# Residual kept scaled by the root of the mean square in the feed-forwards; sum copies placed in the output tile

## The chip, the core and the metric

The kernel runs on one core of a Trainium2 chip. A core has a matrix engine (TensorE, PE in the profile; its weight loads are listed apart as PEld), three engines that work on data in the on-chip memory SBUF (VectorE = DVE, ScalarE = ACT, GpSimd = POOL), and queues that start transfers from the chip's large memory (SP's queue carries most of them here). Matrix products end in a small accumulator memory, PSUM. Each engine takes its instructions strictly in its own order and waits for others through semaphores. The metric is the time of one execution on the device in microseconds (us); the median of several runs counts.

## The reference

The program is an encoder trunk of two layers on 512 tokens with 1024 features, in float32, with 16 learned tokens put in front for the layers and dropped at the end. Each layer adds three things to the residual h:

```python
h = h + 0.5 * swiglu(rmsnorm(h, g[l, 0]), w_gate[l, 0], w_up[l, 0], w_down[l, 0])
h = h + mixer(rmsnorm(h, g[l, 1]), ...)
h = h + 0.5 * swiglu(rmsnorm(h, g[l, 2]), w_gate[l, 1], w_up[l, 1], w_down[l, 1])
...
def rmsnorm(x, g):    # per token
    return x * rsqrt(mean(x * x) + EPS) * g
def swiglu(x, w_gate, w_up, w_down):
    return (silu(x @ w_gate) * (x @ w_up)) @ w_down
```

So there are four feed-forwards (width 2816) and two mixers (a linear-attention branch and a softmax-attention branch, merged by gates). A last rmsnorm gives the output.

## The kernel before

All activations are held transposed: features on the 128 partitions, tokens along the row. The residual `h` is one tile of 8 chunks of 128 features x 528 tokens (512 in the last feed-forward). Every matrix product in full precision is made of three matmuls on halves: each operand is split into a high part (`whi`, `g` and so on) and the rest (`wlo`). For a block of weights ACT makes the high part (L238) and DVE the low part (L239, one instruction of 128x1024).

**The norm.** The gain is multiplied into the operand, but the factor per token, `rs`, is not: products are made from unscaled operands and the factor is put in afterwards. `Norm.rs` (L483) lets PE sum the squares (`means`, L410) and calls `rsqrt_of` (L413), which computes rsqrt with a Newton step; the row `rs` holds -2 times the reciprocal root, hence the factors -0.5 and -0.25 in what follows. Its last two instructions on DVE are L421 and L422.

**A feed-forward** (`ffn`, L507) works through 11 pairs of blocks of 128 hidden features, in three groups of 4, 4 and 3 pairs. For each pair, gate and up products are formed by seven products ("1", "2", "5", "6", "7", "4", "3") in place of eight, each of 24 matmuls of 128x264 (L531), with sums of weight blocks as operands. Those weight sums are made by transfers that add (POOL, L189), fed by loads on SP's queue and, for two of them, by a negation on ACT (L184). The results of the seven products are added up outside PE: ACT copies some PSUM results into a buffer (`snapshot`, L534 to L538, buffer `snap`), DVE adds other PSUM results to them and writes into the tile `c` (L545, L553, L555, L560). `hidden` (L563) then scales gate and up by `rs` (L571; for the up half the scale is left out), takes silu on ACT, multiplies (L577) and splits into `g` high and low (L392, L393).

After each group come the down products (`down`, L580): for each of the 8 chunks of h, matmuls (L404) sum the group's hidden values into PSUM. The up factor was left out, so this sum still lacks one factor per token: `add_to_h` (L496) calls `scaled` (L492, L494), which multiplies PSUM by -0.25 and `rs` into a buffer `t`, and then adds `t` to h (L503). A mixer's output needs no factor and is added straight from PSUM (L499). With the last group's addition a chunk of h is done and the next stage takes it: `chunk` (operand and square, L430 to L442) before a mixer, `pair` (L444) before a feed-forward, `finish_chunk` before the end. Chunks 5 to 7 of the last feed-forward are handled in halves of 256 tokens in `ending` (L1067, L1068).

**Order.** The program is written in a logical order, with weights asked for some products ahead; a scheduler of the framework then fixes the order of instructions on each engine from its own estimates and from priorities. `Norm.rs` runs with high priority. An instruction that needs a buffer waits until the last reader of the buffer's former content is through. Buffers: `g` 16 of 128x528, `t` 6, `rs` 2; for each feed-forward `c` 2 of 128x2112 and `snap` 3 of 128x528; PSUM pools `ss` and `s2` of two tiles each.

Of the kernel before, what the change touches and what calls it, by code (L numbers as in the profile page):

```python
# [17 lines left out]
P = 128  # L18
D = 1024
KC = D // P  # L20
# [255 lines left out]
def build(tc, ctx, xt, wts, win, par, w2, const, umask, out):  # L276
# [10 lines left out]
    slots = {n: pool("s_" + n, b) for n, b in dict(g=16, t=6, rs=2).items()}  # L287
# [27 lines left out]
    def slot(tag, dtype=F32, n=None):  # L315
        return slots[tag].tile([P, T], dtype, tag=tag, name=nm(tag))[:, : n or live[0]]

# [71 lines left out]
    def split(src, tag_hi, tag_lo):  # L389
        n = src.shape[-1]  # L390
        hi, lo = slot(tag_hi, F32R, n), slot(tag_lo, F32R, n)
        S.copy(hi, src)  # L392
        V.tensor_tensor(lo, src, hi.bitcast(F32), ALU.subtract)  # L393
        return hi, lo
# [29 lines left out]
    class Norm:  # L424
# [71 lines left out]
    def add_to_h(m, acc, rs, f):  # L496
        if rs is None:
            for pv, cut in acc.parts:
                V.tensor_tensor(cut(h(m)), cut(h(m)), pv, ALU.add)  # L499
        else:  # L500
            t = slot("t")
            scaled(t, acc, rs, f)
            V.tensor_tensor(h(m), h(m), t, ALU.add)  # L503
# [3 lines left out]
    def ffn(l, f, norm, done, following):  # L507

        x, rs, n = norm.x, None, live[0]
        w = n // 2  # L510
        pools = open_pools("left", psum=("s2",), c=2, snap=3, s2=2)
        made, hid, sums = {}, {}, {}

        def product_of_pair(p, product):
# [19 lines left out]
            def snapshot(name):  # L534
                t = slots["snap"].tile([P, T], F32, tag="snap", name=nm("snap"))[:, :n]
                st[name] = v2(t)
                copied = S.copy(st[name], acc).ins  # L537
                W.behind = copied  # L538

            if product == "1":  # L540
                snapshot("p1")
            elif product == "2":
                c = slots["c"].tile([P, 4 * T], F32, tag="c", name=nm("c"))[:, : 4 * n]
                st["c"] = c.rearrange("p (j q c) -> p j q c", j=2, q=4)
                V.tensor_tensor(st["c"][:, :, 0], st["p1"], acc, ALU.add)  # L545
            elif product == "6":
                snapshot("q")
            elif apart:
                S.copy(st["c"][:, :, 2], acc)
                st["apart"] = True  # L550
            elif product == "7":
                snapshot("r")
                V.tensor_tensor(st["c"][:, :, 3], st["r"], st["Z"][:, :, :w], ALU.add)  # L553
                if "apart" in st:
                    V.tensor_tensor(st["c"][:, :, 2], st["c"][:, :, 2], st["r"], ALU.add)  # L555
                    hidden(st, p, 1)
            elif product == "4":
                hidden(st, p, 1)
            elif product == "3":
                V.tensor_tensor(st["c"][:, :, 1], st["q"], acc, ALU.add)  # L560
                hidden(st, p, 0)

        def hidden(st, p, m):  # L563

            c = st["c"]
            t, u = [c[:, j, 2 * m : 2 * m + 2].rearrange("p q c -> p (q c)") for j in range(2)]
            x21 = st["X"][:, :, :w]
            cuts = [(t, u, t, u, slice(0, n))] if m == 0 or "apart" in st else \
                [(t[:, :w], u[:, :w], x21[:, 0], x21[:, 1], slice(0, w)), (t[:, w:], u[:, w:], t[:, w:], u[:, w:], slice(w, n))]
            for td, _, ts, _, cs in cuts:  # L570
                V.scalar_tensor_tensor(td, ts, -0.5, rs[:, cs], ALU.mult, ALU.mult)  # L571
            act(t, t, AF.Silu)
            if pending:
                with after(prev_act[0]):
                    pending.pop()()
            for _, ud, _, us, cs in cuts:
                V.tensor_tensor(ud, t[:, cs], us, ALU.mult)  # L577
            hid[2 * p + m] = split(u, "g", "g")

        def down(g, m, first, last):  # L580
# [21 lines left out]
        for i, step in enumerate(steps):  # L602
            if step[0] == "P":
# [4 lines left out]
                if step[1:] == (0, "5"):  # L608
                    rs = norm.rs()
# [8 lines left out]
    def project(x, rs, tag, f=1.0, n=T):  # L618
        t = slot(tag, n=n)
# [351 lines left out]
    def mixer(l, norm, done, following):  # L971
# [45 lines left out]
        gates = [project(x, None, "g", n=n_out) for _ in range(EARLY)]  # L1017
        bt = attention(l, x, rs, n_out)
        gates += [project(x, None, "g", n=n_out) for _ in range(2 * KC - EARLY)]
        live[0] = n_out  # L1020
        a = [split(t, "x", "x") for t in sr]
        b = [split(t, "x", "x") for t in bt]
        sig = table("sigmoid_and_others")
        y = []
        for m in range(KC):
# [12 lines left out]
            y.append(split(t, "g", "g"))  # L1038
# [3 lines left out]
        for m in range(KC):  # L1042
            add_to_h(m, product("w_out", Acc(KINDS[m % 4]), y, KC), None, 1.0)
            done(m)
# [12 lines left out]
    def ending(sums, operand, rs):  # L1057
# [144 lines left out]
```

## Time and profile before

| | |
|---|---|
| device time, median of 3 runs | 2235.04 us (2234.63 to 2238.08) |
| span of the profiled execution | 2233.2 us |
| between that span and the median | 1.8 us |
| PE busy | 2196.7 us, 98% |
| DVE busy | 1519.1 us, 68% |
| ACT busy | 1195.1 us, 54% |
| POOL busy | 154.2 us, 7% |
| mean clock granted to PE | 0.998 of full speed |

The profile is of one execution, taken by the hardware; its own device time is its span and what lies around it. Rows of the timeline read: start in us from the begin of the span, duration, engine, line of the kernel, operation, output<-inputs by the program's names (buffer numbers left out), their shapes, how many were merged into the row, and in brackets how long the engine was idle before it and who ended that idle time. Rows of groups give busy us and the mean in ns of one after the bar, then idle us before them. Rows of waits give the waiting engine, tile and line, then whom it waited for, with total us, times and the longest. Rows of stretches give for each engine busy us and the number of its instructions.

Matmuls are pipelined, so a matmul's duration (0.28 us) is longer than the distance from one start to the next (0.12 us).

### The profile page before, as it was taken

Reading aid. Unit: us, or ns where it says so; the run is one execution under the profiler, and the core shown is the slowest. Engines: PE = TensorE matmul, PEld = TensorE weight load, DVE = VectorE, ACT = ScalarE, POOL = GpSimd, SP = SyncE. Lnnn points to the kernel's source line nnn. Section 1 sums busy time; section 2 is a strip of 40 time slices with the busy share of each in tenths; the row PEclk is TensorE's granted clock in tenths of the full one; section 3 lists DMA queues with packets and bytes.
Section 4 is the critical chain, followed back from the end, with each engine's and each line's share of the span. In section 5 each row is a group of like instructions: output and inputs, shape, how many; then the busy total and the mean of one; then the engine's idle time right before and its main releaser. Section 6 shows DMA issues by size and latency. Waiting matters only on the chain.

```text
span 2233.2 us, 39696 instructions
## 1 busy us (share of the span) xinstructions
PE 2196.7 (98%) x16506; PEld 2091.9 (94%) x16506; DVE 1519.1 (68%) x2413; ACT 1195.1 (54%) x1771; POOL 154.2 (7%) x180
## 2 busy tenths in 40 slices
PE   7999999999999999999999999999999999999998
PEld 7999999989999999999999999999788888989897
DVE  7657567586876666565686565675878767756667
ACT  8536355354784564453575353553557836636453
POOL 1111010000000010101011110100000001101010
PEclk9999999999999999999999999999999999999999
DMA  9768563212113486776768686632121146868672
GB/s 275 206 157 221 152 164 106 76 53 72 48 39 114 133 201 168 171 195 154 198 152 207 154 204 167 165 109 77 54 79 48 48 123 156 221 161 207 168 182 67
DMA packets 88612, 315.58 MB, mean 141 GB/s; under 512 B 9840, under 2 KB 12272, under 8 KB 88432
## 3 DMA queue, kind: packets, MB, share of 16 engines
q1 hardware_dynamic: 61136, 218.26, 29.2%
q0 software_dynamic: 25344, 92.29, 23.2%
q8 instruction: 130, 2.13, 0.4%
q10 hardware_dynamic: 1952, 2.50, 0.3%
q14 instruction: 50, 0.41, 0.1%
HBM read 264.77 MB, written 2.10 MB: 120 GB/s over the span
## 4 chain that ended last, share of the span: by engine, by line
PE 79%; DVE 8%; DMA 6%; ACT 5%; issue 2%; SPq 0%; POOL 0%; DVEq 0%; ACTq 0%; POOLq 0%
PE ss L531 30%; PE ss L404 26%; PE mm L404 13%; DMA w<-win 4%; PE sm L404 2%; DVE wlo L239 2%; DMA s<-w 2%; PE sm L916 1%; ACT whi L238 1%; PE ss L891 1%; PE ss L410 1%; ACT t L387 1%; PE sm L932 1%; PE ss L892 1%; PE sm L933 1%
## 5 line engine op out<-in xcount | busy, mean ns | idle before, releaser
L531 PE MATMUL ss<-xc,whi 128*128 128x264 f32 (+1 forms) x4928 | 902.8, 285 | 13.3 <-ACT whi L238 7.4
L531 PEld LDWEIGHTS ss<-xc,whi 128*128 128x128 f32 x4928 | 766.2, 189 | 17.2 <-ACT whi L238 7.6
L531 PE MATMUL ss<-xc,wlo 128*128 128x264 f32 (+1 forms) x2464 | 701.8, 285 | 3.4 <-DVE wlo L239 3.4
L404 PE MATMUL ss<-g,whi 128*128 128x264 f32 (+2 forms) x2692 | 496.8, 300 | 1.6 <-ACT g L392 0.9
L531 PEld LDWEIGHTS ss<-xc,wlo 128*128 128x128 f32 x2464 | 465.7, 189 | 5.2 <-DVE wlo L239 5.0
L404 PEld LDWEIGHTS ss<-g,whi 128*128 128x128 f32 x2692 | 391.6, 188 | 19.1 <-ACT g L392 1.6
L404 PE MATMUL mm<-x,whi 128*128 128x264 f32 (+1 forms) x1712 | 384.7, 315 | 0.0
L239 DVE TENSOR_TENSOR wlo<-w,whi 128x1024 fp32r<-128x1024 f32 (+1 forms) x221 | 268.0, 1217 | 157.2 <-ACT whi L238 157.1
L238 ACT CAST whi<-raw 128x1024 fp32r<-128x1024 f32 x190 | 199.3, 1049 | 246.6 <-PE mm L404 97.5
L238 ACT CAST whi<-w 128x1024 fp32r<-128x1024 f32 (+1 forms) x221 | 229.8, 1046 | 160.0 <-PE ss L404 88.0
L404 PE MATMUL ss<-g,wlo 128*128 128x264 f32 (+2 forms) x1346 | 312.5, 300 | 0.0
L404 PEld LDWEIGHTS mm<-x,whi 128*128 128x128 f32 x1712 | 278.5, 188 | 16.5 <-issue 1.0
L239 DVE TENSOR_TENSOR wlo<-raw,whi 128x1024 fp32r<-128x1024 f32 x190 | 232.0, 1221 | 74.3 <-ACT whi L238 73.9
L404 PE MATMUL mm<-x,wlo 128*128 128x264 f32 (+1 forms) x856 | 266.3, 316 | 0.0
L404 PEld LDWEIGHTS ss<-g,wlo 128*128 128x128 f32 x1346 | 215.8, 188 | 8.2
L537 ACT COPY snap<-ss 128x528 f32<-128x528 f32 (+1 forms) x132 | 78.4, 594 | 221.0 <-PE ss L531 221.0
L404 PEld LDWEIGHTS mm<-x,wlo 128*128 128x128 f32 x856 | 159.7, 188 | 8.4 <-issue 0.7
L494 DVE SCALAR_TENSOR_TENSOR t<-ss,rs 128x528 f32<-128x528 f32 (+1 forms) x93 | 64.5, 701 | 125.5 <-PE ss L404 125.4
L239 DVE TENSOR_TENSOR wlo<-s,whi 128x1024 fp32r<-128x1024 f32 x88 | 107.5, 1222 | 32.9 <-ACT whi L238 32.9
L184 ACT ACTIVATE s<-w 128x1024 f32<-128x1024 f32 x88 | 92.1, 1057 | 53.2 <-DMA w<-win 37.7
L189 POOL DMA_DIRECT2D w<-win x44 | 38.9, 884 | 984.1 <-DMA w<-win 539.9
L238 ACT CAST whi<-s 128x1024 fp32r<-128x1024 f32 x88 | 92.5, 1051 | 0.0
(246 smaller groups left out, 2570.8 us busy)
## 6 DMA issues: line engine op xcount, KB each, us to landing
w<-win SPq DMA_DIRECT2D x219, 512.0 KB, 4.5
raw<-wts SPq DMA_DIRECT2D x190, 512.0 KB, 3.4
s<-win POOLq DMA_DIRECT2D x44, 512.0 KB, 7.1
w<-s POOLq DMA_DIRECT2D x44, 512.0 KB, 5.5
w<-win POOLq DMA_DIRECT2D x44, 512.0 KB, 5.9
s<-w POOLq DMA_DIRECT2D x44, 512.0 KB, 8.0
h<-xt SPq DMA_DIRECT2D x3, 528.0 KB, 6.1
out<-h ACTq DMA_DIRECT2D x4, 256.0 KB, 2.4
```

The source lines that it names most:

```text
L184: self.nc.scalar.activation(t, w, AF.Copy, scale=-1.0)
L189: self.nc.gpsimd.dma_start(t, src, accum_op=ALU.add)
L238: nc.scalar.copy(hi[:, cs], w[:, cs])
L239: nc.vector.tensor_tensor(lo[:, cs], w[:, cs], hi[:, cs].bitcast(F32), ALU.subtract)
L387: prev_act[0] = S.activation(*args, **kw).ins
L404: TE.matmul(acc.half[i][:width], lhs, rhs[:, acc.spans[i]], start=first, stop=last)
L410: TE.matmul(a, weights, x[:, hs], start=True, stop=True)
L494: V.scalar_tensor_tensor(cut(dst[rows]), pv[rows], -0.5 * f, cut(rs[rows]), ALU.mult, ALU.mult)
L531: TE.matmul(acc[:, j], a[:, j, k], b[:, at], start=bool(begin and k == 0 and i == 0), stop=k == len(x) - 1 and i == 2, skip_group_check=no ...
L537: copied = S.copy(st[name], acc).ins
L891: TE.matmul(s[:n, i, :HF], lhs, kh[:, hs], start=True, stop=False)
L892: TE.matmul(s[:n, i, :HF], lhs, kl[:, hs], start=False, stop=True)
```

## The change

Three things are changed.

1. In a feed-forward h is multiplied, before anything is added to it, by the root of the mean square (the inverse of the norm's factor): `Norm.rs(True)` makes a second row `up` = (mean square + EPS) x `rs` with one more DVE instruction, and `down` multiplies each chunk of h by -`up` in the first group. The down sums of all three groups are then added straight from PSUM. After the last group `lower_h` multiplies the chunk by -0.25 `rs`, which gives the residual its own scale back together with the added part. In `ending` the same two steps take the place of scaling and adding.
2. The copies of PSUM sums (`snapshot`) go straight into the parts of the tile `c` that they are to be part of, and the additions happen in place. `c` is now two tiles of 128x1056 for each pair (4 buffers), and `snap` is gone.
3. `g` holds high and low part in one tile of twice the width (8 buffers instead of 16); the mixer's gates use it in the same way.

In the program's order of instructions, the rescalings and the new row stand in the first 25 us or so of each feed-forward, since they need nothing from PE but the mean square. The DVE has 2377 instructions in the program instead of 2405; PE, ACT, POOL have the same number.

```diff
@@ -284,7 +284,7 @@
         return ctx.enter_context(tc.tile_pool(name=name, bufs=bufs, space=space))
 
     one = pool("one", 1)
-    slots = {n: pool("s_" + n, b) for n, b in dict(g=16, t=6, rs=2).items()}
+    slots = {n: pool("s_" + n, b) for n, b in dict(g=8, t=6, rs=2).items()}
     small = pool("small", 4)
     W = Weights(tc, pool("wraw", 3), pool("whi", 4), pool("wlo", 4), wts, win)
     pss = pool("pss", 2, bass.MemoryType.PSUM)
@@ -480,35 +488,40 @@
             if c % 2:
                 self.pair(c // 2)
 
-        def rs(self):
+        def rs(self, root=False):
 
             rs = slot("rs")
             with tc.high_priority():
                 ms = means(o1024, self.acc)
                 with after(table("natural_log_exp_and_others")):
                     rsqrt_of(ms, rs, True)
-            return rs
+                if not root:
+                    return rs
+                (mv, cut), = ms.parts
+                up = slot("rs")
+                V.scalar_tensor_tensor(cut(up), mv, EPS, cut(rs), ALU.add, ALU.mult)
+            return rs, up
 
     def scaled(dst, acc, rs, f, rows=slice(0, P)):
         for pv, cut in acc.parts:
             V.scalar_tensor_tensor(cut(dst[rows]), pv[rows], -0.5 * f, cut(rs[rows]), ALU.mult, ALU.mult)
 
-    def add_to_h(m, acc, rs, f):
-        if rs is None:
-            for pv, cut in acc.parts:
-                V.tensor_tensor(cut(h(m)), cut(h(m)), pv, ALU.add)
-        else:
-            t = slot("t")
-            scaled(t, acc, rs, f)
-            V.tensor_tensor(h(m), h(m), t, ALU.add)
+    def add_to_h(m, acc):
+        for pv, cut in acc.parts:
+            V.tensor_tensor(cut(h(m)), cut(h(m)), pv, ALU.add)
+
+    def lower_h(m, rs, cs=None):
+
+        cs = cs or slice(0, live[0])
+        return V.scalar_tensor_tensor(h(m, cs), h(m, cs), -0.25, rs[:, cs], ALU.mult, ALU.mult)
 
     pending = [load_constants]
 
     def ffn(l, f, norm, done, following):
 
-        x, rs, n = norm.x, None, live[0]
+        x, rs, up, n = norm.x, None, None, live[0]
         w = n // 2
-        pools = open_pools("left", psum=("s2",), c=2, snap=3, s2=2)
+        pools = open_pools("left", psum=("s2",), c=4, s2=2)
         made, hid, sums = {}, {}, {}
 
         def product_of_pair(p, product):
@@ -531,39 +544,43 @@
                         TE.matmul(acc[:, j], a[:, j, k], b[:, at], start=bool(begin and k == 0 and i == 0),
                                   stop=k == len(x) - 1 and i == 2, skip_group_check=not begin)
 
-            def snapshot(name):
-                t = slots["snap"].tile([P, T], F32, tag="snap", name=nm("snap"))[:, :n]
-                st[name] = v2(t)
-                copied = S.copy(st[name], acc).ins
-                W.behind = copied
+            def snapshot(q):
+                W.behind = S.copy(part(st, q), acc).ins
 
             if product == "1":
-                snapshot("p1")
+                st["c"] = [c_tile() for _ in range(2)]
+                snapshot(0)
             elif product == "2":
-                c = slots["c"].tile([P, 4 * T], F32, tag="c", name=nm("c"))[:, : 4 * n]
-                st["c"] = c.rearrange("p (j q c) -> p j q c", j=2, q=4)
-                V.tensor_tensor(st["c"][:, :, 0], st["p1"], acc, ALU.add)
+                V.tensor_tensor(part(st, 0), part(st, 0), acc, ALU.add)
             elif product == "6":
-                snapshot("q")
+                snapshot(1)
             elif apart:
-                S.copy(st["c"][:, :, 2], acc)
+                S.copy(part(st, 2), acc)
                 st["apart"] = True
             elif product == "7":
-                snapshot("r")
-                V.tensor_tensor(st["c"][:, :, 3], st["r"], st["Z"][:, :, :w], ALU.add)
+                snapshot(3)
                 if "apart" in st:
-                    V.tensor_tensor(st["c"][:, :, 2], st["c"][:, :, 2], st["r"], ALU.add)
+                    V.tensor_tensor(part(st, 2), part(st, 2), part(st, 3), ALU.add)
+                V.tensor_tensor(part(st, 3), part(st, 3), st["Z"][:, :, :w], ALU.add)
+                st["r"] = True
+                if "apart" in st:
                     hidden(st, p, 1)
             elif product == "4":
                 hidden(st, p, 1)
             elif product == "3":
-                V.tensor_tensor(st["c"][:, :, 1], st["q"], acc, ALU.add)
+                V.tensor_tensor(part(st, 1), part(st, 1), acc, ALU.add)
                 hidden(st, p, 0)
 
+        def c_tile():
+            return slots["c"].tile([P, 2 * T], F32, tag="c", name=nm("c"))[:, : 2 * n].rearrange(
+                "p (j q c) -> p j q c", j=2, q=2)
+
+        def part(st, q):
+            return st["c"][q // 2][:, :, q % 2]
+
         def hidden(st, p, m):
 
-            c = st["c"]
-            t, u = [c[:, j, 2 * m : 2 * m + 2].rearrange("p q c -> p (q c)") for j in range(2)]
+            t, u = [st["c"][m][:, j].rearrange("p q c -> p (q c)") for j in range(2)]
             x21 = st["X"][:, :, :w]
             cuts = [(t, u, t, u, slice(0, n))] if m == 0 or "apart" in st else \
                 [(t[:, :w], u[:, :w], x21[:, 0], x21[:, 1], slice(0, w)), (t[:, w:], u[:, w:], t[:, w:], u[:, w:], slice(w, n))]
@@ -593,8 +610,11 @@
                     begin=first == 0, end=last == width)
             if last < width:
                 return
-            add_to_h(m, sums[m], rs, 0.5)
+            if g == 0:
+                V.scalar_tensor_tensor(h(m), h(m), -1.0, up, ALU.mult, ALU.mult)
+            add_to_h(m, sums[m])
             if g == len(GROUPS) - 1:
+                lower_h(m, rs)
                 (done or finish_chunk)(m)
 
         steps = ffn_steps((l, f) == (0, 0))
@@ -1063,9 +1090,9 @@
         def chunk(i, c):
             acc, w = sums[c - LATE]
             product("ffn_w_down", acc, operand, len(w), only=i, w=w)
-            t, sq[i] = slot("t")[:, hs[i]], slot("t")[:, hs[i]]
-            V.scalar_tensor_tensor(t, acc.half[i], -0.25, rs[:, hs[i]], ALU.mult, ALU.mult)
-            added = V.tensor_tensor(h(c, hs[i]), h(c, hs[i]), t, ALU.add).ins
+            sq[i] = slot("t")[:, hs[i]]
+            V.tensor_tensor(h(c, hs[i]), h(c, hs[i]), acc.half[i], ALU.add)
+            added = lower_h(c, rs, hs[i]).ins
             if c == KC - 1:
                 ms[i] = pair()[:, 0, : SEQ // 2]
                 TE.matmul(ms[i], o1024, fin.acc[:, hs[i]], start=True, stop=False)
```

What is left out of the diff: `twin`, which makes a `g` tile of double width, its use in `split` and for the gates, and calls whose arguments change with it.

More of the change, by code (lines that the diff above doesn't have):

```diff
@@ L387, in act, with split @@
         prev_act[0] = S.activation(*args, **kw).ins
-    def split(src, tag_hi, tag_lo):
+    def split(src, tag):
         n = src.shape[-1]
-        hi, lo = slot(tag_hi, F32R, n), slot(tag_lo, F32R, n)
+        if tag == "g":
+            both = twin("g", F32R, n)
+            hi, lo = both[:, 0], both[:, 1]
+        else:
+            hi, lo = slot(tag, F32R, n), slot(tag, F32R, n)
         S.copy(hi, src)
@@ L577, in hidden @@
                 V.tensor_tensor(ud, t[:, cs], us, ALU.mult)
-            hid[2 * p + m] = split(u, "g", "g")
+            hid[2 * p + m] = split(u, "g")
         def down(g, m, first, last):
@@ L1016, in mixer, with gate_pairs @@
             gla_pair(l, p, lr, w2t, sr, qa, ka, va, n_out)
-        gates = [project(x, None, "g", n=n_out) for _ in range(EARLY)]
+        gates = []
+        def gate_pairs(n):
+            for _ in range(n):
+                both = twin("g", n=n_out)
+                gates.extend(project(x, None, both[:, i], n=n_out) for i in range(2))
+        gate_pairs(EARLY // 2)
         bt = attention(l, x, rs, n_out)
-        gates += [project(x, None, "g", n=n_out) for _ in range(2 * KC - EARLY)]
+        gate_pairs(KC - EARLY // 2)
         live[0] = n_out
-        a = [split(t, "x", "x") for t in sr]
-        b = [split(t, "x", "x") for t in bt]
+        a = [split(t, "x") for t in sr]
+        b = [split(t, "x") for t in bt]
         sig = table("sigmoid_and_others")
@@ L1037, in mixer @@
             V.tensor_tensor(t, ga, gb, ALU.add)
-            y.append(split(t, "g", "g"))
+            y.append(split(t, "g"))
         close_pools(pools)
```

9 lines of the change are left out of this document (6 added, 3 removed).

## Prediction

> **What bounds the kernel now.** I read the page first: busy shares and the clock granted to TensorE (PE).
>
> ```profile
> PE 2196.7 (98%) x16506; PEld 2091.9 (94%) x16506; DVE 1519.1 (68%) x2413; ACT 1195.1 (54%) x1771; POOL 154.2 (7%) x180
> ...
> PEclk9999999999999999999999999999999999999999
> ```
>
> PE is busy 98% of 2233.2 us at full clock. The change removes no matmul, so it can act only where PE stands still. Next the stretches: 46 to 375 is the first feed-forward (FFN), 796 to 1128 the second, 2200 to 2233 the ending.
>
> ```profile
> core 0: us, PE busy (x) PEld busy (x) DVE busy (x) ACT busy (x) POOL busy (x), PEclk, DMA share, GB/s
> 46.00:375.00 329.00, 328.37 (x2692) 327.90 (x2691) 210.68 (x263) 161.15 (x197) 31.43 (x36) 1.00 0.67 175
> 796.00:1128.00 332.00, 331.12 (x2720) 330.88 (x2719) 210.48 (x272) 166.63 (x205) 36.70 (x42) 1.00 0.73 183
> 2200.00:2233.00 33.00, 23.38 (x152) 20.65 (x150) 25.71 (x54) 7.45 (x15) 0.00 (x0) 0.88 0.19 64
> ```
>
> Column two less column three is PE's idle time: 329.00 - 328.37 = 0.6 us in the first FFN, 332.00 - 331.12 = 0.9 us in the second. VectorE (DVE), which the change relieves, has 329.00 - 210.68 = 118 us free there. PE starts a matmul every 331.12/2720 = 0.122 us. Who makes PE wait at all, over the whole span:
>
> ```profile
> PE ss L531 <- DVE wlo L239: 3.4, 7, 0.7
> PE ss L531 <- ACT snap L537: 2.9, 3, 1.0
> PE ss L404 <- ACT g L392: 0.9, 2, 0.5
> PE ss L404 <- DVE g L393: 0.7, 3, 0.2
> PE ss L531 <- DVE t L494: 0.6, 1, 0.6
> ```
>
> Total us, times, longest. The pair of instructions that the change replaces shows up once, for 0.6 us.
>
> **The change, part by part.** The prices on DVE:
>
> ```profile
> L503 DVE TENSOR_TENSOR h<-h,t 128x528 f32<-128x528 f32 (+1 forms) x93 | 64.5, 702 | 1.6
> L494 DVE SCALAR_TENSOR_TENSOR t<-ss,rs 128x528 f32<-128x528 f32 (+1 forms) x93 | 64.5, 701 | 125.5 <-PE ss L404 125.4
> L499 DVE TENSOR_TENSOR h<-h,ss 128x528 f32<-128x528 f32 (+1 forms) x8 | 5.5, 692 | 0.0
> ```
>
> Scaling out of PSUM, adding from SBUF and adding straight from PSUM all cost 0.70 us. Per FFN and chunk (8 chunks, 4 FFNs) before: three groups of two instructions, 6. After: one rescaling, three additions from PSUM, one scaling down, 5. That saves 32, and 4 new ones make the root of the mean square, so 28 instructions less of some 2400. The ending's last chunks keep their count. 28 x 0.62 us (the distance between neighbours, below) is 17 us of DVE time. DVE is idle before the L494 rows alone for 125.5 us, waiting for the very sums it drains, so the saving is worth nothing by itself; without that idle time it would be worth the PE waits that DVE ends, at most 3.4 + 0.7 + 0.6 by the rows above.
>
> What remains is order. The eight rescalings have no PE result to wait for; in the changed program they stand, with the new instruction, in the first 25 us of each FFN, among the products' work, not in the down sections. This is the second FFN there:
>
> ```profile
> 796.85 1.22 DVE L239 TENSOR_TENSOR wlo<-w,whi 128x1024 fp32r<-128x1024 f32 x1
> 797.99 1.22 DVE L239 TENSOR_TENSOR wlo<-s,whi 128x1024 fp32r<-128x1024 f32 x1
> 800.82 0.70 DVE L553 TENSOR_TENSOR c<-snap,ss 128x528 f32<-128x528 f32 x1 [1.61 <-ACT snap L537]
> 800.84 0.51 PE L531 MATMUL ss<-xc,whi 128*128 128x264 f32 x2 [0.89 <-ACT snap L537]
> ...
> 804.38 1.23 DVE L239 TENSOR_TENSOR wlo<-w,whi 128x1024 fp32r<-128x1024 f32 x1 [1.25 <-ACT whi L238]
> ```
>
> A split weight (wlo) takes DVE 1.2 us and feeds a product of 24 matmuls, 24 x 0.122 = 2.9 us of PE. The wlo made at 796.85 is ready at 798.07 and is read from 800.84: 2.8 us to spare, and 1.61 and 1.25 us of idle DVE follow. The 0.70 us new instruction and the rescalings fit: 0, at worst +1 if a wlo is pushed 1 us past its use. The 0.89 us stall is PE waiting for a copy on ACT that waits for PE; the copy keeps its place and size in the changed program (the output tile takes it instead of a buffer), so those 2.9 us stay. The third and fourth FFN open alike: 0.
>
> The first FFN is tight:
>
> ```profile
> 49.75 0.70 DVE L571 SCALAR_TENSOR_TENSOR c<-c,rs 128x528 f32<-128x528 f32 x1
> 50.37 1.22 DVE L239 TENSOR_TENSOR wlo<-w,whi 128x1024 fp32r<-128x1024 f32 x1
> ...
> 54.89 0.70 DVE L577 TENSOR_TENSOR c<-c 128x528 f32<-128x528 f32 x1
> 55.15 0.86 POOL L189 DMA_DIRECT2D w<-s  x1 [8.31 <-DVE g L393]
> ...
> 58.01 1.22 DVE L239 TENSOR_TENSOR wlo<-w,whi 128x1024 fp32r<-128x1024 f32 x1
> 61.30 0.40 PE L531 MATMUL ss<-xc,whi 128*128 128x264 f32 x2
> ...
> 63.70 1.23 DVE L239 TENSOR_TENSOR wlo<-w,whi 128x1024 fp32r<-128x1024 f32 x1 [0.24 <-ACT whi L238]
> 64.23 0.41 PE L531 MATMUL ss<-xc,whi 128*128 128x264 f32 x2
> ```
>
> A scaling out of SBUF (L571) lets the next one start 0.62 us later, so new instruction and rescalings are 0.7 + 8 x 0.62 = 5.7 us. The wlo at 58.01 (ready 59.23) is read by the third matmul of the product that starts at 61.30, at 61.54: 2.3 us to spare. Putting the changed order on these durations, it is ready about 61.2, so 0.3 us remain. The wlo at 63.70 is ready at 64.93; the changed PE order puts its first matmuls at 64.23 already (before: three us later), which need it at 64.48: 0.4 us late. Queued behind a late wlo on DVE are the sums and splits of hidden values, which PE reads only in the first down section, some 30 us on. A later PE would swallow part of the waits for g (L392, L393: 0.9 and 0.7 us in all). I take +0.3, bounds -0.5 (those stalls shrink) to +2 (the distance is 0.70 and not 0.62, and both wlo slip).
>
> One place where the saving reaches PE is a down section of the last FFN:
>
> ```profile
> 1995.93 0.69 DVE L494 SCALAR_TENSOR_TENSOR t<-ss,rs 128x512 f32<-128x512 f32 x1 [3.02 <-PE ss L404]
> 1996.65 0.69 DVE L503 TENSOR_TENSOR h<-h,t 128x512 f32<-128x512 f32 x1
> 1997.27 1.22 DVE L239 TENSOR_TENSOR wlo<-w,whi 128x1024 fp32r<-128x1024 f32 x1
> ...
> 2069.14 1.23 DVE L239 TENSOR_TENSOR wlo<-w,whi 128x1024 fp32r<-128x1024 f32 x1 [2.77 <-ACT whi L238]
> 2070.42 0.39 PE L531 MATMUL ss<-xc,wlo 128*128 128x256 f32 x1 [0.64 <-DVE wlo L239]
> ```
>
> The wlo at 1997.27 stands behind the pair; it frees a weight buffer that SP's load and then POOL's chain of summing transfers wait for, and that chain is late at 2070.42. One instruction instead of two brings it 0.6 us forward: -0.5, bounds 0 and -1.5 (that 0.64 us and the 0.9 us of the row for g on ACT, if it follows from it).
>
> The entry to the third FFN, where the residual's last chunks set the pace:
>
> ```profile
> 1135.88 1.32 DVE L494 SCALAR_TENSOR_TENSOR t<-ss,rs 128x528 f32<-128x528 f32 x2
> 1136.63 0.51 PE L531 MATMUL ss<-xc,whi 128*128 128x264 f32 x2 [0.62 <-DVE t L494]
> ...
> 1137.72 1.33 DVE L503 TENSOR_TENSOR h<-h,t 128x528 f32<-128x528 f32 x2
> ```
>
> In the last group two instructions per chunk stay two, but the second now stands between the PSUM read and the next chunk. The changed order has the sum of chunk 6 read ahead of two splits, not behind them, so the 0.62 us stall should shrink; chunk 7 ends as late. -0.2, bounds -0.9 to +0.5.
>
> The two mixer starts: before, PE fills the wait for the last normalised chunk with matmuls of the next slab; the changed order issues the 48 of one slab straight and the mean square early.
>
> ```profile
> 375.28 0.65 PE L404 MATMUL ss<-x,whi 128*128 128x264 f32 x4
> 380.23 0.71 DVE L503 TENSOR_TENSOR h<-h,t 128x528 f32<-128x528 f32 x1
> 380.97 0.74 ACT L432 ACTIVATE x<-h,par 128x528 fp32r<-128x528 f32 x1 [2.52 <-DVE h L503]
> 381.75 0.77 DVE L433 SCALAR_TENSOR_TENSOR x<-h,par,x 128x528 fp32r<-128x528 f32 x1 [0.21 <-ACT x L432]
> ```
>
> The slab's first matmul is that at 375.28; the 43rd, 42 x 0.122 later at 380.4, is the first to need chunk 7, whose operand was whole only at 381.75 + 0.77 = 382.5. In the changed order of DVE the chunk's sum is added as soon as PE has it (375.4), then come one wlo (its high half is made by 376.4, so to 377.6), the scaling down (378.3), 0.74 on ACT and 0.77 on DVE: 379.8, in time. -0.3 for the two starts together, since the mean square leaves earlier; if the operand comes no earlier than before, 2 us of stall each: bounds -0.5 to +4.
>
> The ending keeps its two small instructions per half chunk, in the other order; the scaling now stands behind the addition where the transfer out is prepared: +0.2, bounds -0.1 to +0.5.
>
> A rule that speaks against the rescalings in the openings: the Trainium skill, SBUF — State Buffer, section Who interferes with whom, says that a VectorE instruction with two SBUF inputs holds up a GpSimd instruction that reads SBUF, and a rescaling has two such inputs while POOL issues summing transfers there. In the rows above POOL's issue at 55.15 lies wholly under the DVE product of two SBUF operands at 54.89 and takes 0.86 us. By the rule POOL's issues would stretch; by the row they don't, and the sum keeps the row.
>
> Sum: 0.3 + 0 - 0.5 - 0.2 - 0.3 + 0.2 = -0.5 us on the span of 2233.2. The median of the runs, 2235.04, lies 1.8 us above that span; with the same 1.8 the forecast is 2234.5. The lower ends add up to -3.5, the upper ends, with 1 us for each of the three roomy openings, to +10.
>
> **Rivals.** First, slower: the burst in the openings. If nine extra DVE instructions come ahead of a wlo in a block, 5.7 us against 2.3 to 3 us of room, each opening loses 2 us or more and the four give 8: 2243. It decides when the work put ahead of one wlo passes its room. For it: the 0.3 us left in the first FFN. Against it: the changed order spreads the rescalings, four at most in a row, and three openings show idle DVE. Second, slower too: the straight order at the mixer starts, +4, 2238.5. Third, faster: DVE's relief clears every wait of PE for wlo, for g and for L494, 3.4 + 0.9 + 0.7 + 0.6 = 5.6 us: 2229.4. For it: fewer instructions in the down sections. Against it: most of these waits sit at openings and transitions, where the count rises or stays. Fourth, the change does nothing that PE sees, down to the order: 2235.0. Fifth, POOL is held by the rescalings, as two inputs in SBUF would make it: two 0.70 us delays per opening for its chain, of which the first and last FFN have no room, +2.8, 2237.8; the row at 55.15 speaks against it.
>
> **How the numbers follow.** What three runs of this kernel can tell from no change is about 0.2%, 4.5 us: faster is below 2230.6, slower above 2239.5. Chances: forecast with the fourth case 0.58; burst 0.14; mixer starts 0.08; relief 0.16; POOL 0.04. Faster takes half of the relief and some of the forecast's lower tail and of a lucky median, 0.18; slower takes the burst and part of the mixer case (with a delay elsewhere), 0.20; 0.62 remains. The range runs from 2230.4, most of the relief, to 2240.5, which holds the mixer case, POOL and the burst's milder half.
>
> **What would show it.** PE idle in 46 to 375 near 1 us; the rescalings at 0.70 us apiece within 25 us of the four new instructions; PE's waits for wlo between 3 and 5 us in all; the 2.9 us behind the copies unchanged; the stall at 1136 smaller; no PE gap at the mixer starts above 0.5 us. I am wrong if wlo waits rise by more than 4 us, if a gap of 2 us opens at a mixer start, or if PE's matmuls change their pace, which none of these steps foresees.

## The result and the profile after

The kernel after takes 2239.55 us (median of 14 runs, 2236.46 to 2244.81), the kernel before on the same chip 2235.39 us (14 runs): the ratio is 1.002, with a 95% interval of 1.0012 to 1.0028, that is 2.7 to 6.3 us slower. The forecast was 2234.5 us and no measurable change. The profiled execution after has a span of 2236.5 us, 3.3 us more than that of before.

The page after, busy shares and granted clock; then the same stretches as in the prediction; then who makes PE wait:

```profile
PE 2200.3 (98%) x16506; PEld 2096.7 (94%) x16506; DVE 1499.8 (67%) x2385; ACT 1194.6 (53%) x1771; POOL 154.3 (7%) x180
...
PEclk9999999999999999999999999999999999999999
```

```profile
46.00:375.00 329.00, 328.92 (x2690) 328.70 (x2690) 207.42 (x259) 162.17 (x199) 32.24 (x37) 1.00 0.68 174
796.00:1128.00 332.00, 330.50 (x2707) 330.19 (x2706) 201.66 (x255) 165.77 (x203) 37.55 (x44) 1.00 0.72 183
```

```profile
PE ss L544 <- ACT c L548: 3.8, 3, 1.6
PE ss L544 <- DVE wlo L239: 3.3, 6, 0.7
PE ss L544 <- DVE h L511: 1.8, 1, 1.8
```

DVE does 28 instructions less (2413 to 2385) and 19.3 us less work, and PE takes longer all the same. In the first feed-forward PE now stands still for 329.00 - 328.92 = 0.1 us, half a microsecond less than before; in the second for 1.5 us, 0.6 more. Waits for the copies grew from 2.9 to 3.8 us. But look at the first row again: the busy time of PE rose by 3.6 us with the same 16506 matmuls, while its idle time (span less busy) went from 36.5 to 36.2 us. So between these two executions the loss is not standing still. About half of it is the pace of matmuls. The chain of waits tells where: it lists stretches in which PE runs one kind of matmul after another with no wait between them (start, duration, tile and line, how many). The down matmuls of each group and the output product stand there, before:

```profile
112.46 38.11 PE ss L404 x312
241.22 37.64 PE ss L404 x312
388.06 5.89 PE mm L404 x48
731.33 5.83 PE ss L404 x48
871.32 37.99 PE ss L404 x312
1000.00 37.65 PE ss L404 x312
1230.31 37.89 PE ss L404 x312
1358.82 37.91 PE ss L404 x312
1965.25 36.22 PE ss L404 x156
2091.49 36.17 PE ss L404 x156
```

and after:

```profile
112.55 38.30 PE ss L412 x312
241.56 38.31 PE ss L412 x312
389.23 5.88 PE mm L412 x48
734.49 5.89 PE ss L412 x48
875.63 38.09 PE ss L412 x312
1004.44 38.16 PE ss L412 x312
1235.32 38.12 PE ss L412 x312
1364.12 38.09 PE ss L412 x312
1971.31 35.96 PE ss L412 x156
2095.46 35.95 PE ss L412 x156
```

Two readings. The durations: six stretches of 312 matmuls of 264 columns took 227.19 us together and now take 229.07, 122.4 ns a matmul against 121.4; the two stretches of 512 columns became faster, 72.39 to 71.91 us. The starts: the distance from row to row, after less before, shows where 3.3 us went.

| from row to row (before) | after less before | what is in it |
|---|---|---|
| start to 388.06, first feed-forward | +1.2 | pace +0.9 |
| 388.06 to 731.33, first mixer | +2.0 | a stretch at half the clock, +1.6 (below) |
| 731.33 to 871.32, output product and second opening | +1.2 | pace +0.5 (the six like rows behind 731.33 went from 5.79 to 5.87), PE's gap at the opening +0.6 |
| 871.32 to 1230.31 | +0.7 | pace +0.6, the entry to the third feed-forward +0.7, smaller waits -0.3, the rest not assigned |
| 1230.31 to 1965.25 | +1.1 | pace +0.4, gap at the fourth opening +0.6 |
| 1965.25 to 2091.49 | -2.1 | pace -0.3, the stalls at 2070 and 2077 (0.64 and 0.53) gone, -0.6 not assigned |
| 2091.49 to the end | -0.7 | pace -0.2, PE's idle time -0.4 |

The mixer's row is the other half. The page gives PEclk in tenths for slices of 56 us, and a short dip doesn't show there. A narrow stretch of the profile after shows it; the second row has the same place in `up_late`, a run further below whose program is the kernel after in every engine's order (columns as in the prediction's stretches; PEclk is third from the end):

```profile
569.71:573.12 3.41, 3.41 (x17) 3.34 (x18) 1.94 (x6) 1.10 (x4) 0.00 (x0) 0.50 0.00 0
571.25:574.66 3.41, 3.41 (x31) 3.41 (x31) 3.01 (x10) 2.44 (x6) 0.00 (x0) 1.00 0.00 0
```

For 3.41 us the granted clock is 0.50, 17 matmuls fall into the stretch in place of 31, and what follows starts 1.6 us later. Six of the 14 profiles have this dip between 568 and 575 us (the kernel after, `after_again`, `g_only`, `scale_c`, `mended`, `mended_shift`), and their first mixer takes 344.7 to 345.4 us; the other eight don't, and take 343.3 to 343.9. One program runs with and without it, so these 1.6 us are no fixed cost of the change. What brings the dip is not shown. Pace (1.9 us over all rows) and dip (1.6) make up PE's 3.6 us.

### The profile page after: what moved, and what is told of

The parts are those of the page before. It is cut to its first block, busy times and chain, and to the rows that moved or that the text cites. A ratio compares the mean times of both kernels' runs of the same rounds, so it can differ in the third digit from the quotient of the medians.

```text
span 2236.5 us, 39655 instructions
## 1 busy us (share of the span) xinstructions
PE 2200.3 (98%) x16506; PEld 2096.7 (94%) x16506; DVE 1499.8 (67%) x2385; ACT 1194.6 (53%) x1771; POOL 154.3 (7%) x180
## 4 chain that ended last, share of the span: by engine, by line
PE 79%; DVE 9%; DMA 5%; ACT 4%; issue 2%; POOL 0%; SPq 0%; DVEq 0%; ACTq 0%; POOLq 0%
PE ss L544 31%; PE ss L412 26%; PE mm L412 13%; DMA w<-win 3%; PE sm L412 2%; DVE wlo L239 2%; DMA s<-w 1%; PE sm L936 1%; ACT whi L238 1%; PE ss L911 1%; ACT t L391 1%; PE ss L418 1%; PE sm L952 1%; PE sm L953 1%; PE ss L912 1%
## 5 line engine op out<-in xcount | busy, mean ns | idle before, releaser
L548 ACT COPY c<-ss 128x528 f32<-128x528 f32 (+1 forms) x132 | 78.5, 594 | 219.5 <-PE ss L544 219.4
L511 DVE TENSOR_TENSOR h<-h,ss 128x528 f32<-128x528 f32 (+1 forms) x101 | 70.2, 697 | 140.3 <-PE ss L412 140.0
L184 ACT ACTIVATE s<-w 128x1024 f32<-128x1024 f32 x88 | 92.7, 1058 | 82.6 <-DMA w<-win 67.2
```

The source lines that it names most:

```text
L184: self.nc.scalar.activation(t, w, AF.Copy, scale=-1.0)
L548: W.behind = S.copy(part(st, q), acc).ins
```

## The experiments

Two theories on what the change itself costs. Pace: the wide `g` tiles put the operand of the down matmuls at other addresses, and PE reads it more slowly. Order: the scaling's instructions delay something that PE needs. All times are medians; "before" is the kernel before on the same chip.

**The parts apart, and both kernels again** (before 2234.29 us, 35 runs). `g_only` is the kernel before with the wide tiles and nothing else:

```diff
-    slots = {n: pool("s_" + n, b) for n, b in dict(g=16, t=6, rs=2).items()}
+    slots = {n: pool("s_" + n, b) for n, b in dict(g=8, t=6, rs=2).items()}
...
-        hi, lo = slot(tag_hi, F32R, n), slot(tag_lo, F32R, n)
+        if tag == "g":
+            both = twin("g", F32R, n)
+            hi, lo = both[:, 0], both[:, 1]
```

`scale_c` is the kernel after with `g` as before: scaling and copies, without the wide tiles. `before_again` and `after_again` are the two kernels once more.

> The kernel before with one part of the change alone: g in one tile of double width (8 buffers). Theory G (the layout of g changes PE's pace where g is the moving operand): the six stretches of 312 down matmuls in the chain of waits, 227.2 us in all before and 229.1 us after, take 228.8 to 229.4 us here, and the time is 2 to 4 us over the kernel before. Rival W (the wait of PE at the openings, +2.0 us in three gaps, comes from the rescalings and costs the time): 227.2 us in those stretches and the time of the kernel before within 1 us. Rival N (the pace is chance of one execution): the stretches land anywhere from 227 to 229.5, unlike both.

> The changed kernel without the wide g tiles: residual scaled and copies in the output tile, g as 16 separate buffers. Theory G: the six stretches of 312 matmuls take 226.9 to 227.6 us, and the time is within 1.5 us of the kernel before. Rival W: the gaps of PE of 1.5, 1.8 and 1.6 us at the openings of the second, third and fourth feed-forward stay, and the time stays 3 to 5 us over the kernel before.

> The kernel before, unchanged, profiled in another execution. Theories G and W: the six stretches of 312 matmuls repeat to 0.05 us each (38.11, 37.64, 37.99, 37.65, 37.89, 37.91). Rival N: they move by 0.2 us or more each. Time as the kernel before, within 1 us.

> The changed kernel, unchanged, profiled in another execution. Theories G and W: the six stretches repeat (38.30, 38.31, 38.09, 38.16, 38.12, 38.09, each within 0.05 us), PE's gaps at the openings of the second to fourth feed-forward are again 1.5 to 1.8 us. Rival N: the stretches move by 0.2 us or more. Time 3 to 5 us over the kernel before.

Measured: `g_only` 2237.47 us, ratio 1.0013 [1.0005, 1.0022]; `scale_c` 2237.65 us, 1.0014 [1.0006, 1.0023]; `before_again` 2235.14 us, 1.0 [0.9991, 1.0009]; `after_again` 2237.94 us, 1.0019 [1.001, 1.0027]. So each part alone costs some 3 us. That the two together cost 3.7 and not 6.5 is within what intervals of 2 us to each side allow. For `g_only` both the stretches and the time came as theory G expected. For `scale_c` only the stretches did: its time is not within 1.5 us of the kernel before, and it has the gaps that the rival names (1.51, 1.50 and 1.59 us). Neither theory alone is the whole.

The clock has a share in these medians too. The mean granted clock of each execution was 0.9978 on average over the 59 executions of the kernel after, `after_again`, `up_late`, `g_only` and `scale_c`, 0.9982 over 112 of the kernel before. One dip as above lowers the mean by 0.0008 (half of 3.41 in 2236 us) and costs 1.6 us, so the difference of 0.0004 is worth some 0.8 us, an estimate from these figures. The profiled execution of `after_again`, 2244.67 us, has three dips, at 42, 571 and 1189 us. Whether the slower kernels have more such dips, and why, stays open.

The six stretches settle the pace: they are the same to 0.01 us in every execution of one arrangement of `g` and follow that arrangement (`xc64`, a later run in which other tiles lie elsewhere too, differs from `after_shift` by up to 0.03 us a stretch). In the table, the start of the high part is taken from the addresses in the built programs; each stretch reads eight tiles of `g`.

| kernel | six stretches of 312, us | sum | high part of `g`, bytes beyond a multiple of 128 |
|---|---|---|---|
| before, `scale_c` | 38.11 37.64 37.99 37.65 37.89 37.91 | 227.19 | first feed-forward: all at 64, then all at 0; second: 6 of 8 at 64, then 2; third: 4 of 8, twice |
| after, `g_only`, `up_late`, `mended` | 38.30 38.31 38.09 38.16 38.12 38.09 | 229.07 | 64 |
| `before_shift` | 37.78 38.12 37.79 38.09 37.97 37.87 | 227.62 | 0 and 64 exchanged |
| `after_shift`, `g_shift` | 37.61 37.62 37.78 37.90 37.88 37.84 | 226.63 | 0 |

**Addresses** (before 2235.16 us, 33 runs). If the start counts and not the width, a tile of 64 bytes ahead of `g` must mend it, and one behind `g` keeps all later buffers where they were modulo 128:

```diff
-    slots = {n: pool("s_" + n, b) for n, b in dict(g=8, t=6, rs=2).items()}
+    slots = {}
+    for n, b in dict(pad=1, g=8, pad2=1, t=6, rs=2).items():
+        slots[n] = pool("s_" + n, b)
+        if n.startswith("pad"):
+            V.memset(slots[n].tile([P, 16], F32, tag=n, name=n), 0.0)
```

> The kernel after, with a small tile of 64 bytes a partition put in the on-chip memory ahead of the g buffers and one behind them, so that every high part of g starts at a multiple of 128 bytes (in the kernel after it starts 64 bytes beyond one, in the kernel before by turns at one and 64 bytes beyond). Nothing else changes; the order of the instructions is that of the kernel after. Theory A, the pace of the down matmuls hangs on where the high part of g starts: the six stretches of 312 down matmuls of 528 tokens, 229.07 us together in the kernel after and 227.19 in the kernel before, fall to about 226 (37.6 to 37.7 each), the stretches of 48 output matmuls from 5.87 to 5.79, and the time by some 2.5 to 4 us against the kernel after. Theory B, it is the wide tile itself (high and low part 2112 bytes apart in one buffer): the six stretches stay at 229.1 and the time stays that of the kernel after.

> The kernel before with the same two small tiles around its g buffers, so that the buffers whose high part started at a multiple of 128 bytes now start 64 bytes beyond one and the others the other way round. Theory A: the stretches of 312 down matmuls change places, those of 37.64 us rise and those of 37.9 to 38.1 fall, each by 0.2 us or more, and the sum, 227.19 us, changes by less than 1 us. Theory B: no stretch moves by more than 0.05 us, since no tile is wide. Both: the time within 1.5 us of the kernel before.

`after_shift` takes 2234.26 us, 0.9997 [0.9988, 1.0006]: the loss is gone with no change in the order of one matmul. `before_shift` takes 2234.38 us, 0.9997 [0.9989, 1.0006]. The chain of waits of `after_shift`, then of `before_shift`:

```profile
111.84 37.61 PE ss L416 x312
239.94 37.62 PE ss L416 x312
```

```profile
111.27 37.78 PE ss L408 x312
239.62 38.12 PE ss L408 x312
```

In `before_shift` the first two stretches change places, 38.11 to 37.78 and 37.64 to 38.12, and so do those of the second feed-forward; the two of the third move by less than 0.1 us. The expectation, which took 64 and 0 to alternate everywhere, didn't foresee that; the addresses in the table do, since the shift exchanges four tiles for four there. The small tiles also move the weights by 128 bytes, but within the kernel before, where no tile of any kind is shifted, the first two stretches differ by 0.47 us all the same. The rival (the wide tile itself) falls as the cause of the loss: the tiles of `after_shift` are as wide. Yet the start is not all: with all eight tiles at 64 a stretch takes 38.11 us with narrow tiles and 38.30 with wide ones. The expected 37.6 to 37.7 for all six was met by the first two only, the others stay at 37.8 to 37.9; and the six rows of the output product fell from 5.87 to 5.83 us, not to 5.79.

Beside them ran `up_late`, meant to move the new instruction (root of the mean square) out of the high-priority block, and `both`, the two edits together.

```diff
-                if not root:
-                    return rs
-                (mv, cut), = ms.parts
-                up = slot("rs")
-                V.scalar_tensor_tensor(cut(up), mv, EPS, cut(rs), ALU.add, ALU.mult)
+            if not root:
+                return rs
+            (mv, cut), = ms.parts
+            up = slot("rs")
+            V.scalar_tensor_tensor(cut(up), mv, EPS, cut(rs), ALU.add, ALU.mult)
```

> The kernel after with the one new instruction per feed-forward that makes the root of the mean square taken out of the high-priority block, so that it no longer stands between two weight splits on DVE at the second and fourth feed-forward's opening. Theory, the new instruction is what makes PE wait longer there, by way of the weight split, the negation on ACT that needs it and the copy queued behind that: PE's gaps, 1.50 us at 803.7 and 1.59 us at 1901.4 in the kernel after, go back to some 0.9 and 1.0 us, the time falls by 1.2 us, and the stretches of 312 down matmuls stay at 229.1 us in all. Rival, the copies themselves are later because they now write into the output tile: the gaps stay at 1.5 and 1.6 us.

> The two edits before together: the kernel after with the high parts of g at multiples of 128 bytes and the new instruction out of the high-priority block. If both theories hold, the pace of the down matmuls (about 226 us for the six stretches) and the two openings (0.9 and 1.0 us) are both mended, and the time is 4 to 5 us below the kernel after and 1 to 3 us below the kernel before, some 2232 us where the kernel before takes 2234.3. If neither holds it is the time of the kernel after.

2238.39 us, 1.0018 [1.0008, 1.0029], and 2234.79 us, 0.9999 [0.999, 1.0008]. The gaps stayed at 1.48 and 1.60 us, but this says nothing for the rival: the scheduler put the instruction back to its old place, so `up_late` is the kernel after in every engine's order and `both` is `after_shift`. They serve as repeats: `up_late` is the one that shows the kernel after without the dip of the clock in the first mixer, and `after_shift` lies 4.1 us below it.

**The opening.** The timeline of the kernel after, second feed-forward:

```profile
801.73 0.70 DVE L502 SCALAR_TENSOR_TENSOR rs<-ss,rs 128x528 f32<-128x528 f32 x1
...
802.34 1.22 DVE L239 TENSOR_TENSOR wlo<-s,whi 128x1024 fp32r<-128x1024 f32 x1
...
803.59 1.06 ACT L184 ACTIVATE s<-w 128x1024 f32<-128x1024 f32 x1 [2.52 <-DVE wlo L239]
...
804.56 0.58 ACT L548 COPY c<-ss 128x528 f32<-128x528 f32 x1
...
805.19 0.51 PE L544 MATMUL ss<-xc,whi 128*128 128x264 f32 x2 [1.50 <-ACT c L548]
```

and before, beside the rows that the prediction shows:

```profile
799.24 1.06 ACT L184 ACTIVATE s<-w 128x1024 f32<-128x1024 f32 x1 [1.90 <-DVE wlo L239]
...
800.21 0.58 ACT L537 COPY snap<-ss 128x528 f32<-128x528 f32 x1
```

The new instruction (L502) stands between two weight splits. The second split ends 0.6 us later, ACT's negation (L184) waits for it, the copy is queued behind the negation, and PE waits for the copy: 1.50 us in place of 0.89. `mended` issues the row only after that copy in the scheduler's order, which puts it behind the second split, and at the entry to the third feed-forward it adds the down sums first:

```diff
+                if step[1:] == (0, "7"):
+                    up = make_up(W.behind)
...
-            add_to_h(m, sums[m])
+            with tc.high_priority() if g == len(GROUPS) - 1 and (l, f) == (0, 1) else nullcontext():
+                add_to_h(m, sums[m])
```

`mended_shift` adds the two small tiles to it, `g_shift` is `g_only` with the two small tiles, and `xc64` is `mended_shift` with 96 bytes more in each tile of the operand `xc` (before 2235.67 us, 33 runs).

> The kernel after with two orders mended: the instruction that makes the root of the mean square is issued only after the copy of product 7 of a feed-forward's first pair (so it stands behind the weight split that the negation on ACT needs, at the second and fourth opening), and at the entry to the third feed-forward the additions out of PSUM go ahead of the scalings down and of the new operand's splits. Theory: PE's gaps of 1.50 us at 804 and 1.59 us at 1901 go back to 0.9 and 1.0 us and the gap of 1.79 us at 1141 falls to some 0.6 us, together 2.4 us less standing still, while the six stretches of 312 down matmuls stay at 229.07 us; the time falls by some 2 us against the kernel after, to about 2236 where the kernel before takes 2235. Rival: the copy on ACT is late for another reason (the transfers, or its target in the output tile), and the gaps at 804 and 1901 stay at 1.5 and 1.6 us.

> The kernel after with both orders mended and with the small tiles that put the high parts of g at multiples of 128 bytes. If the loss is pace and order, and nothing else, the six stretches take 226.6 us, the three gaps some 2.4 us less than in the kernel after, and the time is 4.5 to 6.5 us below the kernel after and 1 to 3 us below the kernel before.

> The kernel before with the wide g tiles alone, and with the small tiles that put every high part of g at a multiple of 128 bytes: nothing of the scaling or of the copies is in it, so no opening and no entry changes. Theory A (address): the six stretches fall from 227.19 us in the kernel before and 229.07 with wide tiles alone to some 226.6, and the time is 0.5 to 2.5 us below the kernel before, where the wide tiles alone were 3 us above it. Theory B (the wide tile is slow in itself): the stretches at 229.1, the time 3 us above the kernel before.

> The kernel of mended_shift with 96 bytes more in each tile of the products' operand xc, so that high and low part of a block stand 64 bytes apart modulo 128 (as with g) instead of 32. It asks whether the rule found for g holds for the products too. If the distance of high and low part is what counts, the stretches of 600 product matmuls fall from 73.2 us by 0.5 us or more each; if what counts is only where the high part starts, the pace of a product changes with its block but the sum stays; if it is a matter of the down matmuls alone, the stretches stay at 73.2 us within 0.05.

`mended`: 2238.21 us, 1.0011 [1.0002, 1.002]. Its timeline at the same place:

```profile
802.57 1.22 DVE L239 TENSOR_TENSOR wlo<-s,whi 128x1024 fp32r<-128x1024 f32 x1
803.71 0.70 DVE L504 SCALAR_TENSOR_TENSOR rs<-ss,rs 128x528 f32<-128x528 f32 x1
803.82 1.06 ACT L184 ACTIVATE s<-w 128x1024 f32<-128x1024 f32 x1 [1.90 <-DVE wlo L239]
...
804.79 0.58 ACT L553 COPY c<-ss 128x528 f32<-128x528 f32 x1
...
805.42 0.52 PE L549 MATMUL ss<-xc,whi 128*128 128x264 f32 x2 [0.89 <-ACT c L553]
```

The gap is back at 0.89 us, at the fourth opening at 0.99, though the copy still goes into the output tile: the order was the cause, and the rival falls. At the third feed-forward the edit failed: PE's waits for the copies fell by 1.1 us, and those for weight splits rose by 2.6, part of it at the entry:

```profile
PE ss L549 <- DVE wlo L239: 5.9, 10, 1.2
PE ss L549 <- ACT c L553: 2.7, 3, 1.0
```

The expected 2 us were therefore not seen as time: the ratio 1.0011 doesn't stand apart from 1.002.

`mended_shift` takes 2233.19 us, 0.999 [0.9982, 0.9999], 2.5 us below the kernel before, as expected, though of its three gaps only two shrank (0.88 and 1.00 us; the third is 1.55). `g_shift` takes 2232.11 us, 0.9983 [0.9975, 0.9992], the fastest of all: 3.6 us below the kernel before, a microsecond more than expected. Wide tiles at the right address are thus a gain, without scaling and copies: 0.6 us of it is the six stretches and 1.2 the stalls at 2070 and 2077, which are gone; the rest is not assigned. `xc64`, 2235.68 us, 0.9998 [0.9989, 1.0007], gains nothing: its stretches of 600 product matmuls take 73.12 us where `mended_shift` has 73.00. None of its three readings fits, so no run here shows that what was found for `g` holds for the products.

## Why the prediction was wrong

**The step that failed first** is the sentence behind the busy shares: "The change removes no matmul, so it can act only where PE stands still." It made PE's pace a constant. The last sentence on what would prove it wrong named a change of pace, "which none of these steps foresees"; that is what happened. The wide tiles stand in the diff, and I took them for bookkeeping. They cost 1.9 us in the six stretches and 0.5 us in the output product, and gave 0.5 us back in the last feed-forward. The clock's dip, 1.6 us in the profile after, was not foreseen either; another execution of the same program lacks it. The terms of the sum, all on standing still, came to about nothing together (36.5 to 36.2 us of idle PE), which is close to the -0.5 forecast, but by luck: most of them were wrong one by one, as follows.

**The openings, costed at 0.** The room was counted from the split to PE's reading of it (2.8 us), and the idle DVE was there. The chain that ran out of room was another: split, negation on ACT, copy behind it in ACT's order, PE. "Those 2.9 us stay" failed with it: 3.8 us, 0.6 each at the second and fourth opening, 0.3 less at the third.

**The first opening** (+0.3, bounds from -0.5): PE's idle time fell by 0.5 us there, and the stretch to 112 us grew by 0.1. The rescalings keep 0.62 us apart, as taken:

```profile
56.54 2.56 DVE L614 SCALAR_TENSOR_TENSOR h<-h,rs 128x528 f32<-128x528 f32 x4
...
57.67 0.87 POOL L189 DMA_DIRECT2D w<-win  x1 [1.12 <-DMA w<-win]
```

The second row bears on the rule cited there (the Trainium skill, SBUF — State Buffer, Who interferes with whom): a transfer's issue on POOL lies wholly under four instructions with two SBUF inputs and still takes 0.87 us. The rival "POOL held" is out: POOL is busy 154.3 us, before 154.2. The choice was right, but the row it rested on didn't carry it: the product at 54.89 ends at 55.59 and the issue only at 56.01, so about half of it lay under the product. That an issue on POOL is a reader of the kind the rule names was the prediction's own assumption; no hold-up shows.

**The entry to the third feed-forward** (-0.2): wrong in sign.

```profile
1139.96 0.69 DVE L511 TENSOR_TENSOR h<-h,ss 128x528 f32<-128x528 f32 x1
1140.58 1.32 DVE L464 TENSOR_TENSOR xc<-t,xc 128x528 fp32r<-128x528 f32 x2
1141.82 0.70 DVE L516 SCALAR_TENSOR_TENSOR h<-h,rs 128x528 f32<-128x528 f32 x1
1142.44 0.69 DVE L511 TENSOR_TENSOR h<-h,ss 128x528 f32<-128x528 f32 x1
...
1143.18 0.51 PE L544 MATMUL ss<-xc,whi 128*128 128x264 f32 x2 [1.79 <-DVE h L511]
```

Before, two PSUM reads stood back to back (the row at 1135.88). Now the read of the next chunk stands behind two splits and the scaling of the chunk ahead, and PE waits 1.79 us in place of 0.62 and 0.52. I had seen that chunk 6's sum moves ahead of the splits, and not followed the read of chunk 7, which frees the accumulator that PE needs.

**The stall at 2070** (-0.5): it vanished, but not for the reason given. `scale_c` has the one instruction in place of two and keeps the stall; `g_only` has the old two and loses it. How the wide tiles remove it was not followed. The row of `scale_c`:

```profile
2073.76 0.39 PE L536 MATMUL ss<-xc,wlo 128*128 128x256 f32 x1 [0.76 <-DVE wlo L239]
```

**The mixer starts** (-0.3): no gap above 0.5 us, as forecast; what the straight order gained there was not measured apart. **The ending** (+0.2): the part from 2091 on became 0.7 us shorter, 0.2 of it pace. **DVE's relief**, 19.3 us less work, was worth nothing that PE shows, as argued.

The burst in the openings came nearest among the slower rivals, but not with its size or place: it foresaw 2 us at each opening from a late operand of PE; there were 0.6 us at two of them, from a late copy.

## What to carry to other kernels

When a change touches how tiles are cut or pooled, compare the operands' addresses before and after, and read the pace of long unbroken stretches: 0.8% of pace in the down matmuls (1.9 us) was worth three of the 0.6 us stalls found here. When an instruction is put into a full queue, follow everything that waits for what stands behind it, on every engine, up to PE; room up to PE's own reading of the result is not enough. And an order mended at one place can hand its gain to the next wait, so look at all of PE's waits, not at the gap that was mended. Last, one profile is one execution: before a difference is put down to the change, read the granted clock in short stretches where the two part, since a dip of 3.41 us was worth as much as the pace.

## What the runs showed of the hardware

The pace of the fp32 matmul stream depends on where the moving operand lies. In the first feed-forward 312 matmuls of 264 columns take 37.61 us with the high part at a multiple of 128 bytes (120.5 ns each) and 38.30 us 64 bytes beyond (122.8 ns); in the third the same two placements differ by 0.24 us only (37.88 and 38.12). At 512 columns it is the other way round, 36.2 us against 35.95 for 156. The Trainium skill, TensorE: Matmul & The Clock Gate, section Back-to-back issue gap, gives N/2.4 + 2.5 ns for the isolated gap at full clock, with no address in it; for 264 columns that would be 112.5 ns, an estimate from its formula, and every stretch of 264 columns here is slower.

Something else in the placement counts too. With the small tiles the weights' tiles lie 128 bytes further on, the same modulo 128, and the products' moving operand `xc` lies where it was. Yet a stretch of 600 product matmuls falls, from the kernel before to `g_shift`:

```profile
150.57 73.19 PE ss L531 x600
```

```profile
149.97 73.00 PE ss L543 x600
```

Every kernel with these tiles and `xc` as it was shows 73.00 to 73.02. Which of the moved tiles does it, and why the third feed-forward answers so much less than the first, were not tried further.

The clock granted to PE can halve for 3.41 us while PE is busy: 0.50 from 569.71 us in the profile after, with matmuls of 264 columns starting 0.22 us apart in place of 0.12, and not at that place in another execution of the same program.
